# Four edits to a planned two-layer decoder trunk: parameters added later, 32 warm-ups, a cast on VectorE, a lead of 50 for three modulation vectors

## The chip, the cores and the metric

The kernel runs on one core of a Trainium2 chip. The core has five engines with queues of their own: TensorE (PE, matmuls; its weight loads are listed as PEld), VectorE (DVE), ScalarE (ACT), GpSimd (POOL) and SyncE (SP), which here issues nearly all transfers from the main memory. The metric is the device time of one execution in microseconds; the median of three runs is compared.

## The reference, cut to what matters

One sequence of 256 tokens of width 1024 passes through two layers. Each layer is a half-step SwiGLU feed-forward (width 2816), a mixer, and a second half-step feed-forward. Every sublayer is normalised and modulated by vectors that come from the conditioning vector c; a last norm follows.

```
for l in range(2):
    mod = (silu(c) @ w_mod[l] + b_mod[l]).reshape(9, 1024)         # nine modulation vectors
    h = rmsnorm(x, g[l, 0]) * (1 + mod[1]) + mod[0]
    x = x + 0.5 * mod[2] * swiglu(h, w_ffn1_gu[l], w_ffn1_down[l])
    h = rmsnorm(x, g[l, 1]) * (1 + mod[4]) + mod[3]
    x = x + mod[5] * hybrid_mixer(h, w_in[l], w_out[l], ...)
    h = rmsnorm(x, g[l, 2]) * (1 + mod[7]) + mod[6]
    x = x + 0.5 * mod[8] * swiglu(h, w_ffn2_gu[l], w_ffn2_down[l])
return rmsnorm(x, g_final)
```

The mixer projects h once and feeds three parts: windowed attention (8 query heads, 2 key/value heads, window 128), a gated linear recurrence behind a convolution of 4, and a gated convolution of 3, sb * conv3(sc * sx). Their outputs are concatenated and projected back. All data are float32.

## The kernel before

x is kept transposed, as `xT`, 8 tiles of 128 channels by 256 tokens. Every weight tile is loaded as float32 into a buffer `raw` (three of them) and split in two by `unit` (line 323): ACT casts it to the high half `wH` (line 336), DVE subtracts to get the remainder `wL` (line 341). Eight such pairs can be held (`"w": 8`). The activations are split the same way into `zH`, `zL`, so one product takes three matmuls (`mm3`, lines 348 to 350), or two where both halves of the activation are streamed at once (`mm2`, lines 355 and 356). The weights of a feed-forward come in 11 chunks of 256 columns for gate and up; the first three chunks of the first feed-forward are taken row by row together with the first two modulation vectors, by `first`. `evac` (line 473) and the lines 505 to 518 turn a result into the SwiGLU product; `x_add` (line 491) adds a sublayer's output to x; `make_z` (413, 416) makes the next input. At the end of each sublayer but the last, `stats` (line 445) puts four small matmuls on PE that sum the squares.

A modulation vector is made by `mod_vector`: eight transfers of 512 KB into `mraw` (three buffers), a DVE step for each (lines 373 and 375) into the one buffer `macc`, a reduction (line 379), four small matmuls (line 384) and a last addition (line 387). Vectors 0 and 1 of layer 0 are made by `first` instead; the other 16 are made by this function, in the order of their numbers, since `macc` is one buffer. Of layer l vector 5 gates the mixer's output, 6 and 7 are the shift and scale behind the mixer.

The mixer's convolution part ends in the tile `sp`; its product with sb (line 731) is split into `yo`: a cast on ACT (line 834) and a subtraction on DVE (line 835). These are the last halves that the output projection takes.

`consts` loads the mixers' parameters: seven small transfers (sinks, convolution weights, biases, lambda; `ssum_t` and `sinkb`, line 884) and eight for the block-diagonal gate matrices (`gatew`, line 1048), with a clearing of the gate matrices (line 1040), copies of the position bias on ACT (1052) and some 30 tiny DVE operations for a softplus.

Before the data arrive, `N_WARM` matmuls of a tile of ones run on PE (line 924); each shows as two instructions.

The order of the work on each engine is not written by hand. Every operation is added to a planner with its engine, an estimated duration, what it reads and writes, and for PE the sum of the matmul time added before it (`base`). `due` walks back from the end and gives each operation the latest start `lst` at which nothing behind it is late; `lead` is taken off it. `emit` then simulates the engines: of all operations that are ready and have a buffer it takes the engine that can start first, and on it, of those that start within 0.06 us of the earliest, the one with the smallest `lst`:

```
soon = [c for c in cand if c[0] <= t0 + EAGER]
t1, o = min(soon, key=lambda c: (c[1].lst + 2.0 * (c[0] - t0), c[1].idx))
```

A transfer of over 300 KB is a candidate only once the modelled wire is at most `BACKLOG` = 4 us behind. The order so found is the program order of each engine; on the chip an engine works through it in that order.

Of the kernel before, what the change touches and what calls it, by code (L numbers as in the profile page):

```python
# [8 lines left out]
F32 = mybir.dt.float32  # L9
F32R = mybir.dt.float32r  # L10
ACTF = mybir.ActivationFunctionType
ALU = mybir.AluOpType
# [13 lines left out]
LAT = {("PE", "PE"): 0.002, ("DVE", "DVE"): 0.128, ("ACT", "ACT"): 0.143, ("POOL", "POOL"): 0.1, ("PE", "DVE"): 0.196,  # L26
       ("PE", "ACT"): 0.197, ("DVE", "PE"): 0.177, ("ACT", "PE"): 0.217, ("DVE", "ACT"): 0.128, ("ACT", "DVE"): 0.131,
       ("DVE", "POOL"): 0.2, ("POOL", "DVE"): 0.06}
MOD_LEAD = 8.0
EAGER = 0.06  # L30
MARGIN = 1.0
HOLD = 40.0
LAGS = (0, 1, 5)
BACKLOG = 4.0
N_WARM = 40


class T:
# [15 lines left out]
class Plan:  # L54
# [6 lines left out]
    def add(self, eng, dur, fn, r=(), w=(), base=None, kb=0, lead=0.0):  # L61
        o = Op()
        o.eng, o.dur, o.fn, o.kb, o.idx, o.lead = eng, dur, fn, kb, len(self.ops), lead
        deps, tiles = set(), []
        for key in list(r) + list(w):
            t = key[0] if isinstance(key, tuple) else key
            if isinstance(t, T) and t not in tiles:
                tiles.append(t)
                if not t.ops and not t.loose:
                    self.order.setdefault(t.tag, []).append(t)  # L70
                t.ops.append(o)
        for key in r:
            assert key in self.lastw or key in ("zsH", "zsL") or key[0] == "zS", key
            if key in self.lastw:
                deps.add(self.lastw[key])
            self.readers.setdefault(key, []).append(o)
        for key in w:
            if key in self.lastw:
                deps.add(self.lastw[key])
            deps.update(self.readers.get(key, ()))  # L80
            self.lastw[key] = o
            self.readers[key] = []
        deps.discard(o)
        o.deps, o.tiles = deps, tiles
        if eng == "PE" and base is None:
            o.base = self.pe
            self.pe += dur
        else:
            o.base = base
        self.ops.append(o)  # L90
        return o
# [107 lines left out]
def cd(n):  # L199
    return 0.068 + n / 960.0  # L200


def ca(n, p=0):
    return 0.093 + n / 1200.0 + 0.093 * p
# [3 lines left out]
def trunk(ctx: ExitStack, tc: tile.TileContext, x, c, w_mod, b_mod, g_norm, w_gu1, w_dn1, w_gu2, w_dn2,  # L208
# [6 lines left out]
    V, A, G, PE = nc.vector, nc.scalar, nc.gpsimd, nc.tensor  # L215
    P = Plan()
    add = P.add
# [28 lines left out]
    bT = const.tile([128, NL, 72], F32, name="bT")  # L246
    cact = const.tile([128, KD], F32, name="cact")
    c32 = const.tile([128, KD, 32], F32, name="c32")
    mod = const.tile([128, NL, 72], F32, name="mod")
# [38 lines left out]
    def l_cols(w, l, col):  # L288
        raw = load([(ALLP, v_kc, w[l, :, col:col + 256].rearrange("(k p) c -> p k c", p=128))])
        return [(raw, lambda r, t=t: v_kc(r)[:, :, t * 128:t * 128 + 128], KD, None) for t in range(2)]  # L290
# [70 lines left out]
    def mcol(l, v):  # L361
        return mod[:, l, v * 8:v * 8 + 8]

    def mod_vector(l, v):
        acc, t32, ps = new("macc"), new("t32"), new("s", loose=True)
        for k in range(KD):
            raw = new("mraw")
            add("SP", 0.06, lambda k=k, raw=raw: nc.sync.dma_start(out=raw(), in_=w_mod[l, k * 128:k * 128 + 128, v * D:v * D + D]),
                w=[raw], kb=524.0)

            def go(k=k, raw=raw):
                if k == 0:
                    V.tensor_scalar(out=acc(), in0=raw(), scalar1=cact[:, k:k + 1], scalar2=None, op0=ALU.mult)
                else:
                    V.scalar_tensor_tensor(out=acc(), in0=raw(), scalar=cact[:, k:k + 1], in1=acc(), op0=ALU.mult, op1=ALU.add)  # L375
            add("DVE", 0.66 if k == 0 else 1.2, go, r=[raw, "c"] + ([acc] if k else []), w=[acc])

        def red():
            V.tensor_reduce(out=t32(), in_=acc().rearrange("p (b c) -> p b c", c=32), axis=AX.X, op=ALU.add, apply_transpose=True)

        def mm():
            tv = t32().rearrange("p (k b) -> p b k", b=4)
            for b in range(4):
                PE.matmul(ps()[32 * b:32 * b + 32, 0:8], lhsT=fold, rhs=tv[:, b, :], start=True, stop=True, skip_group_check=True)

        def fin():
            V.tensor_tensor(out=mcol(l, v), in0=ps()[:, 0:8], in1=bT[:, l, v * 8:v * 8 + 8], op=ALU.add)
        add("DVE", 1.14, red, r=[acc], w=[t32])
        add("PE", 0.1, mm, r=[t32, "fold"], w=[ps], base=1e9)
        add("DVE", 0.08, fin, r=[ps, "bT"], w=[("mod", l, v)], lead=MOD_LEAD)  # L390


    def prep(l, s):
# [101 lines left out]
    def ffn(l, s, wg, wd, getR, nxt, first=False, done=None):  # L495
# [27 lines left out]
        for ch in range(11):  # L523
            if first and ch < 3:
                if ch:
                    continue
                pss, prods = [new("gu") for _ in range(3)], {}
                for k in range(KD):
                    if k % 2 == 0:
                        first(k // 2, prods)  # L530
                        if k == 4:
                            R = getR()
                    ws = [unit(u) for u in l_rows(wg, l, k)]
                    for m in range(6):
                        def go(m=m, k=k, ws=ws, pss=pss):
                            for i in range(2):
                                mm3(pss[m // 2]()[:, m % 2, i * S:i * S + S], ws[i], m, zH[:, k, 0:S], zL[:, k, 0:S],
                                    k == 0 and i == 0, k == KD - 1)
                        prods[k, m] = add("PE", 2 * C3, go, r=[(w, j) for w in ws for j in range(2)] + [("zH", k), ("zL", k)],
                                          w=[(pss[m // 2], m % 2)])  # L540
                consts()
                for m in range(6):
                    put(m, pss[m // 2], R, m % 2)
                continue
            ug, uu = l_cols(wg, l, ch * 256), l_cols(wg, l, FF + ch * 256)
            for t in range(2):
                m = ch * 2 + t
                ps = pair([unit(ug[t]), unit(uu[t])])
                if R is None:
                    R = getR()  # L550
                put(m, ps, R)
# [3 lines left out]
            r=[("mod", l, 3 * s + 2)], w=[gv])  # L555
        a = prep(*nxt) if nxt else None
        ssum = new("ssum")
        for dp in range(4):
            pss = [new("gu"), new("gu")]
            f0 = 0  # L560
            for ci, n in enumerate((8, 8, 6)):
                us = l_down(wd, l, f0, n, dp * 256)
                for t in range(2):
                    w, ps = unit(us[t]), pss[t]
# [22 lines left out]
    def mixer(l, getR, nxt):  # L587
# [13 lines left out]
        ps = P2(l_cols(w_in, l, 512))  # L601
# [148 lines left out]
        for g in range(2):  # L750
            ps = new("s")
# [55 lines left out]
        sp = new("big")  # L807
# [23 lines left out]
        for i in range(2):  # L831
            add("DVE", 0.4, lambda i=i, t=t: stt(sp()[:, 2 + i, :], t()[:, i, 0:S], t()[:, i, 256:257], sp()[:, 2 + i, :], ALU.add, ALU.mult),
                r=[t], w=[(sp, 2 + i)])
        add("ACT", ca(512), lambda: A.copy(yo()[:, 0, 0:2, :], sp()[:, 2:4, :]), r=[(sp, 2), (sp, 3)], w=[(yo, 0, 0)])  # L834
        add("DVE", cd(512), lambda: V.tensor_tensor(out=yo()[:, 1, 0:2, :], in0=sp()[:, 2:4, :], in1=yo().bitcast(F32)[:, 0, 0:2, :],  # L835
                                                    op=ALU.subtract), r=[(sp, 2), (sp, 3), (yo, 0, 0)], w=[(yo, 1, 0)])

        acc = [new("gu"), new("gu")]

# [255 lines left out]
    fin = {}  # L1095
# [27 lines left out]
    add("ACT", ca(256), lambda: A.copy(RM(), psm()[:, 0:256]), r=[psm], w=[RM], base=E0)  # L1123

    for l, v in [(0, v) for v in range(2, 9)] + [(1, v) for v in range(9)]:
        mod_vector(l, v)
    s0 = ffn(0, 0, w_gu1, w_dn1, lambda: spread(r0, True), (0, 1), first=first)
    s1 = mixer(0, lambda: spread(stats(s0)), (0, 2))
    s2 = ffn(0, 2, w_gu2, w_dn2, lambda: spread(stats(s1)), (1, 0))
# [61 lines left out]
```

## Time and profile before

| | |
|---|---|
| median of 3 runs | 976.43 us (974.82 to 977.58) |
| profiled execution | 980.18 us, span 978.4 us |
| PE busy | 959.5 us, 98% of the span |
| PE weight loads busy | 907.1 us, 93% |
| DVE busy | 803.5 us, 82% |
| ACT busy | 501.1 us, 51% |
| moved from main memory | 240.52 MB, 247 GB/s over the span |

Matmuls are pipelined, so a PE that shows as busy may still be waiting a little; the number of matmuls that a stretch starts tells more than its busy time. The times of rows count from the start of the span. In a timeline row the first number is the start, the second the duration, and what stands in brackets is how long the engine had been idle and what ended that. The granted clock of PE stands as a share of full speed.

### The profile page before, as it was taken

The page shows a single profiled execution, that of the slowest core. Times are in us where ns is not written, and L with a number is a line of the kernel's source. Part 1 is how long each engine was busy: PE and PEld are TensorE (multiplying, and loading weights), DVE is VectorE, ACT ScalarE, POOL GpSimd, SP SyncE. Part 2 cuts the span into 40 slices and gives each one's busy share as a digit, 9 for nine tenths or more (in the row PEclk, how much of TensorE's full clock was granted, in tenths as well). Part 3 has the DMA queues.
Part 4 walks back from the last instruction along what each step waited for, and adds up shares of the span by engine and source line. Part 5 has one row for each costly group of instructions (what it writes and reads, how often), then busy time and mean ns, then how long its engine had stood idle before and what let it go on. Part 6 is the DMA issues. An engine that isn't in the chain of part 4 may idle for free.

```text
span 978.4 us, 18188 instructions
## 1 busy us (share of the span) xinstructions
PE 959.5 (98%) x7407; PEld 907.1 (93%) x7407; DVE 803.5 (82%) x1211; ACT 501.1 (51%) x773; POOL 11.4 (1%) x16
## 2 busy tenths in 40 slices
PE   8999999999999999999999999999999999999997
PEld 7889999889888999998899999988998999999886
DVE  5688999999899999989789976677999989666651
ACT  4436554445955554544454554444577555544431
POOL 1000000000000000000000000000000000000000
PEclk9999999999999999999999999999999999999999
DMA  9976789998856889997878965598784777656521
GB/s 329 348 254 225 262 294 328 345 306 307 206 174 236 295 272 325 306 319 252 297 226 295 309 205 182 194 314 252 251 233 172 254 246 247 208 183 192 164 76 44
DMA packets 185783, 242.75 MB, mean 248 GB/s; under 512 B 6504, under 2 KB 164452, under 8 KB 185700
## 3 DMA queue, kind: packets, MB, share of 16 engines
q1 hardware_dynamic: 185160, 240.96, 75.3%
q8 instruction: 58, 0.95, 0.4%
q10 hardware_dynamic: 540, 0.63, 0.2%
q14 instruction: 25, 0.20, 0.1%
HBM read 240.52 MB, written 1.05 MB: 247 GB/s over the span
## 4 chain that ended last, share of the span: by engine, by line
PE 88%; DVE 7%; DMA 3%; issue 1%; ACT 0%; ACTq 0%; DVEq 0%; POOLq 0%
PE gu L348 20%; PE gu L350 20%; PE gu L349 20%; PE gu L356 15%; PE gu L355 8%; DMA mraw_t<-in_w_mod_dram 2%; DVE wL L341 2%; DVE macc_t L375 1%; DVE xT L491 1%; PE s L986 1%; PE gu L924 1%; DMA sq_t<-in_b_mod_dram 1%; DVE hp_t L731 1%; DMA raw_t<-in_w_ffn_gu_dram 1%; DVE big_t L657 0%
## 5 line engine op out<-in xcount | busy, mean ns | idle before, releaser
L348 PE MATMUL gu<-zH,wH 128*128 128x258 f32 (+1 forms) x1664 | 473.4, 284 | 2.7 <-DVE ev_t L473 1.9
L336 ACT CAST wH<-raw_t 128x1024 fp32r<-128x1024 f32 (+1 forms) x324 | 320.3, 1015 | 301.1 <-PE gu L356 114.8
L350 PE MATMUL gu<-zH,wL 128*128 128x258 f32 (+1 forms) x1664 | 471.1, 283 | 1.2 <-DVE wL L341 1.2
L349 PE MATMUL gu<-zL,wH 128*128 128x258 f32 (+1 forms) x1664 | 469.4, 282 | 0.7 <-DVE zL L416 0.3
L341 DVE TENSOR_TENSOR wL<-raw_t,wH 128x1024 fp32r<-128x1024 f32 (+1 forms) x324 | 375.1, 1181 | 56.3 <-ACT wH L336 54.8
L348 PEld LDWEIGHTS gu<-zH,wH 128*128 128x128 f32 x1664 | 315.3, 189 | 6.2 <-issue 2.5
L349 PEld LDWEIGHTS gu<-zL,wH 128*128 128x128 f32 x1664 | 315.6, 190 | 2.0 <-DVE zL L416 1.5
L350 PEld LDWEIGHTS gu<-zH,wL 128*128 128x128 f32 x1664 | 314.5, 189 | 1.6 <-DVE wL L341 1.6
L356 PE MATMUL gu<-hp_t,wH 128*128 128x512 f32 x704 | 248.0, 393 | 0.0
L355 PE MATMUL gu<-hp_t,wL 128*128 128x256 f32 x704 | 200.4, 285 | 1.8 <-DVE xT L491 1.8
L356 PEld LDWEIGHTS gu<-hp_t,wH 128*128 128x128 f32 x704 | 132.2, 188 | 29.7
L375 DVE SCALAR_TENSOR_TENSOR macc_t<-mraw_t,cact,macc_t 128x1024 f32<-128x1024 f32 x112 | 143.3, 1279 | 6.9 <-DMA mraw_t<-in_w_mod_dram 6.6
L355 PEld LDWEIGHTS gu<-hp_t,wL 128*128 128x128 f32 x704 | 132.3, 188 | 2.5 <-PE gu L356 1.2
L473 DVE TENSOR_TENSOR ev_t<-gu,Rb 128x514 f32<-128x514 f32 x98 | 67.6, 690 | 47.9 <-PE gu L350 47.2
L517 ACT CAST hp_t<-h_t 128x256 fp32r<-128x256 f32 x88 | 35.5, 405 | 73.8 <-DVE h_t L515 73.8
L513 ACT ACTIVATE sg_t<-ev_t 128x256 f32<-128x256 f32 x88 | 44.1, 502 | 41.4 <-DVE ev_t L473 33.2
L491 DVE SCALAR_TENSOR_TENSOR xT<-gu,gv_t,xT 128x256 f32<-128x256 f32 x80 | 36.8, 479 | 17.6 <-PE gu L356 16.0
L518 DVE TENSOR_TENSOR hp_t<-h_t,hp_t 128x256 fp32r<-128x256 f32 x88 | 36.9, 420 | 8.9 <-ACT hp_t L517 8.5
L515 DVE SCALAR_TENSOR_TENSOR h_t<-ev_t,sg_t 128x256 f32<-128x256 f32 x88 | 41.7, 475 | 0.8 <-ACT sg_t L513 0.5
L349 PE MATMUL gu<-hp_t,wH 128*128 128x256 f32 x128 | 36.9, 288 | 1.8 <-DVE hp_t L835 1.8
L348 PE MATMUL gu<-hp_t,wH 128*128 128x256 f32 x128 | 37.8, 295 | 0.2 <-ACT hp_t L834 0.2
L350 PE MATMUL gu<-hp_t,wL 128*128 128x256 f32 x128 | 36.7, 286 | 0.0
(168 smaller groups left out, 487.7 us busy)
## 6 DMA issues: line engine op xcount, KB each, us to landing
raw_t<-in_w_ffn_gu_dram SPq DMA_DIRECT2D x82, 1024.0 KB, 7.2
mraw_t<-in_w_mod_dram SPq DMA_DIRECT2D x128, 512.0 KB, 5.6
raw_t<-in_w_ffn_down_dram SPq DMA_DIRECT2D x32, 1024.0 KB, 5.3
raw_t<-in_w_ffn_down_dram SPq DMA_DIRECT2D x16, 768.0 KB, 6.3
raw_t<-in_w_in_dram SPq DMA_DIRECT2D x12, 1024.0 KB, 5.8
hp_t<-in_w_mod_dram SPq DMA_DIRECT2D x8, 1024.0 KB, 10.8
raw_t<-in_w_ffn_gu_dram SPq DMA_DIRECT2D x16, 384.0 KB, 8.9
raw_t<-in_w_in_dram SPq DMA_DIRECT2D x8, 512.0 KB, 7.0
```

The source lines that it names most:

```text
L336: A.copy(dst(0), view(raw()))
L341: V.tensor_tensor(out=dst(1), in0=view(raw()), in1=h, op=ALU.subtract)
L348: PE.matmul(ps, lhsT=wh[:, wi, :], rhs=aH, start=first, stop=False, skip_group_check=True)
L349: PE.matmul(ps, lhsT=wh[:, wi, :], rhs=aL, start=False, stop=False, skip_group_check=True)
L350: PE.matmul(ps, lhsT=wl[:, wi, :], rhs=aH, start=False, stop=last, skip_group_check=True)
L355: PE.matmul(ps[:, 0:S], lhsT=wl[:, wi, :], rhs=a[:, 0, :], start=first, stop=False, skip_group_check=True)
L356: PE.matmul(ps, lhsT=wh[:, wi, :], rhs=a, start=False, stop=last, skip_group_check=True)
L375: V.scalar_tensor_tensor(out=acc(), in0=raw(), scalar=cact[:, k:k + 1], in1=acc(), op0=ALU.mult, op1=ALU.add)
L473: V.tensor_tensor(out=t()[:, :, 0:257], in0=ps()[:, :, 0:257], in1=Rb[:, R, 0:257].unsqueeze(1).to_broadcast([128, 2, 257]), op=ALU.mult)
L491: add("DVE", 0.4, lambda: V.scalar_tensor_tensor(out=xT[:, d, :], in0=src(), scalar=gv()[:, d:d + 1], in1=xT[:, d, :], op0=ALU.mult, op1=A ...
L513: add("ACT", ca(S, 1), lambda: A.activation(out=sg(), in_=t()[:, 0, 0:S], func=ACTF.Silu, bias=bg_()), r=[t], w=[sg])
L515: add("DVE", 0.4, lambda: V.scalar_tensor_tensor(out=h(), in0=t()[:, 1, 0:S], scalar=bu_(), in1=sg(), op0=ALU.add, op1=ALU.mult), r=[t, sg ...
```

## The change

`consts()` is called before chunk 7 of the first feed-forward's gate and up weights, not after the first three chunks, so its operations are added later and its due times are later by the matmul time of the four chunks between. `N_WARM` falls from 40 to 32. In the mixer the cast of the convolution half moves from ACT to DVE, as a copy that is planned together with the subtraction behind it as one operation, `cut`. `mod_vector` gets its lead as an argument: 50 for the vectors 5, 6 and 7 of both layers, 8 as before for the others.

```diff
--- before.py
+++ after.py
@@ -26,13 +26,13 @@
 LAT = {("PE", "PE"): 0.002, ("DVE", "DVE"): 0.128, ("ACT", "ACT"): 0.143, ("POOL", "POOL"): 0.1, ("PE", "DVE"): 0.196,
        ("PE", "ACT"): 0.197, ("DVE", "PE"): 0.177, ("ACT", "PE"): 0.217, ("DVE", "ACT"): 0.128, ("ACT", "DVE"): 0.131,
        ("DVE", "POOL"): 0.2, ("POOL", "DVE"): 0.06}
-MOD_LEAD = 8.0
+MOD_LEAD, AHEAD = 8.0, 50.0
 EAGER = 0.06
 MARGIN = 1.0
 HOLD = 40.0
 LAGS = (0, 1, 5)
 BACKLOG = 4.0
-N_WARM = 40
+N_WARM = 32
 
 
 class T:
@@ -361,7 +361,7 @@
     def mcol(l, v):
         return mod[:, l, v * 8:v * 8 + 8]
 
-    def mod_vector(l, v):
+    def mod_vector(l, v, lead):
         acc, t32, ps = new("macc"), new("t32"), new("s", loose=True)
         for k in range(KD):
             raw = new("mraw")
@@ -387,7 +387,7 @@
             V.tensor_tensor(out=mcol(l, v), in0=ps()[:, 0:8], in1=bT[:, l, v * 8:v * 8 + 8], op=ALU.add)
         add("DVE", 1.14, red, r=[acc], w=[t32])
         add("PE", 0.1, mm, r=[t32, "fold"], w=[ps], base=1e9)
-        add("DVE", 0.08, fin, r=[ps, "bT"], w=[("mod", l, v)], lead=MOD_LEAD)
+        add("DVE", 0.08, fin, r=[ps, "bT"], w=[("mod", l, v)], lead=lead)
 
 
     def prep(l, s):
@@ -538,10 +538,11 @@
                                     k == 0 and i == 0, k == KD - 1)
                         prods[k, m] = add("PE", 2 * C3, go, r=[(w, j) for w in ws for j in range(2)] + [("zH", k), ("zL", k)],
                                           w=[(pss[m // 2], m % 2)])
-                consts()
                 for m in range(6):
                     put(m, pss[m // 2], R, m % 2)
                 continue
+            if first and ch == 7:
+                consts()
             ug, uu = l_cols(wg, l, ch * 256), l_cols(wg, l, FF + ch * 256)
             for t in range(2):
                 m = ch * 2 + t
@@ -831,9 +832,10 @@
         for i in range(2):
             add("DVE", 0.4, lambda i=i, t=t: stt(sp()[:, 2 + i, :], t()[:, i, 0:S], t()[:, i, 256:257], sp()[:, 2 + i, :], ALU.add, ALU.mult),
                 r=[t], w=[(sp, 2 + i)])
-        add("ACT", ca(512), lambda: A.copy(yo()[:, 0, 0:2, :], sp()[:, 2:4, :]), r=[(sp, 2), (sp, 3)], w=[(yo, 0, 0)])
-        add("DVE", cd(512), lambda: V.tensor_tensor(out=yo()[:, 1, 0:2, :], in0=sp()[:, 2:4, :], in1=yo().bitcast(F32)[:, 0, 0:2, :],
-                                                    op=ALU.subtract), r=[(sp, 2), (sp, 3), (yo, 0, 0)], w=[(yo, 1, 0)])
+        def cut():
+            V.tensor_copy(yo()[:, 0, 0:2, :], sp()[:, 2:4, :])
+            V.tensor_tensor(out=yo()[:, 1, 0:2, :], in0=sp()[:, 2:4, :], in1=yo().bitcast(F32)[:, 0, 0:2, :], op=ALU.subtract)
+        add("DVE", 2 * cd(512), cut, r=[(sp, 2), (sp, 3)], w=[(yo, 0, 0), (yo, 1, 0)])
 
         acc = [new("gu"), new("gu")]
 
@@ -1123,7 +1125,7 @@
     add("ACT", ca(256), lambda: A.copy(RM(), psm()[:, 0:256]), r=[psm], w=[RM], base=E0)
 
     for l, v in [(0, v) for v in range(2, 9)] + [(1, v) for v in range(9)]:
-        mod_vector(l, v)
+        mod_vector(l, v, AHEAD if v in (5, 6, 7) else MOD_LEAD)
     s0 = ffn(0, 0, w_gu1, w_dn1, lambda: spread(r0, True), (0, 1), first=first)
     s1 = mixer(0, lambda: spread(stats(s0)), (0, 2))
     s2 = ffn(0, 2, w_gu2, w_dn2, lambda: spread(stats(s1)), (1, 0))
```

## Rows read from the trace of the kernel before

**Rows 1.** Busy time by engine in two stretches; clock, DMA share and GB/s last

```profile
...
100.00:125.00 25.00, 25.00 (x211) 25.00 (x210) 23.46 (x30) 12.95 (x19) 0.00 (x0) 1.00 0.88 291
...
250.00:275.00 25.00, 23.14 (x178) 20.71 (x177) 22.42 (x60) 24.28 (x60) 0.00 (x0) 1.00 0.64 173
```

**Rows 2.** The chain that ended last: the matmuls of `stats`

```profile
...
226.81 0.34 PE s L445 x4
...
317.82 0.34 PE s L445 x4
...
700.13 0.34 PE s L445 x4
...
784.82 0.34 PE s L445 x4
```

**Rows 3.** Timeline of 262 to 266 us

```profile
...
263.67 1.28 DVE L375 SCALAR_TENSOR_TENSOR macc_t<-mraw_t,cact,macc_t 128x1024 f32<-128x1024 f32 x1 [2.58 <-DMA mraw_t<-in_w_mod_dram]
...
265.61 0.39 PE L348 MATMUL gu<-zH,wH 128*128 128x258 f32 x1 [1.86 <-DVE ev_t L473]
```

**Rows 4.** Timeline of 299 to 305 us

```profile
...
301.18 2.35 DVE L341 TENSOR_TENSOR wL<-raw_t,wH 128x1024 fp32r<-128x1024 f32 x2
...
301.29 0.62 ACT L834 CAST hp_t<-big_t 128x512 fp32r<-128x512 f32 x1 [1.33 <-DVE big_t L731]
...
303.45 0.68 DVE L835 TENSOR_TENSOR hp_t<-big_t,hp_t 128x512 fp32r<-128x512 f32 x1
...
304.19 0.39 PE L349 MATMUL gu<-hp_t,wH 128*128 128x256 f32 x1 [1.84 <-DVE hp_t L835]
```

**Rows 5.** PE alone in stretches of 2 us: busy, granted clock, DMA share

```profile
...
8.00:10.00 2.00, 1.00 (x10) 1.00 1.09 335
...
66.00:68.00 2.00, 2.00 (x12) 0.52 1.07 374
...
304.00:306.00 2.00, 1.81 (x11) 0.75 0.62 203
306.00:308.00 2.00, 2.00 (x12) 0.50 1.00 339
```

**Rows 6.** Timeline of PE near 64 us

```profile
...
64.43 0.38 PE L348 MATMUL gu<-zH,wH 128*128 128x258 f32 x1 [0.85 <-ACT wH L336]
...
65.69 0.38 PE L350 MATMUL gu<-zH,wL 128*128 128x258 f32 x1 [0.76 <-DVE wL L341]
```

**Rows 7.** Timeline of SP's queue, 45 to 66 us

```profile
...
47.39 1.44 SPq L884 DMA_DIRECT2D ssum_t<-in_lru_conv_w_dram  x1
...
57.80 0.40 SPq L272 DMA_DIRECT2D raw_t<-in_w_ffn_gu_dram  x1
58.24 1.36 SPq L1048 DMA_DIRECT2D gatew<-in_lru_gate_a_w_dram  x2
```

**Rows 8.** What SP's queue waited for, 45 to 70 us: total, times, longest

```profile
...
SPq L884 <- DMA mraw_t<-in_w_mod_dram: 3.5, 2, 2.5
```

**Rows 9.** Timeline of the first 20 us

```profile
...
1.99 0.91 DVE L1040 MEMSET gatew<- 128x1024 f32 x1 [0.16 <-issue]
...
15.64 3.62 PE L924 MATMUL gu<-ones 128*128 128x128 f32 x30
...
17.83 1.82 DVE L341 TENSOR_TENSOR wL<-raw_t,wH 128x768 fp32r<-128x768 f32 x2
...
19.34 0.47 PE L348 MATMUL gu<-zH,wH 128*128 128x256 f32 x1
```

**Rows 10.** Groups by line and shape: busy and mean ns, idle time before

```profile
...
L336 ACT CAST wH<-raw_t 128x1024 fp32r<-128x1024 f32 x276 | 280.6, 1047 | 231.0 <-PE gu L349 79.5 <-PE gu L356 68.7 <-DMA raw_t<-in_w_ffn_gu_dram 51.9
...
L1017 DVE CAST zH<-h_t 128x256 fp32r<-128x256 f32 x8 | 2.4, 295 | 0.3
```

**Rows 11.** Timeline of DVE: the reductions of layer 0's vectors 5 and 7

```profile
...
234.82 1.24 DVE L379 TRANSPOSE_TENSOR_REDUCE t_t<-macc_t 128x32 f32<-128x1024 f32 x1
...
296.68 1.25 DVE L379 TRANSPOSE_TENSOR_REDUCE t_t<-macc_t 128x32 f32<-128x1024 f32 x1
```

## The prediction

> **What bounds the kernel now.** I first read the table of stretches. From 75 us on, in most stretches, TensorE (PE) starts 211 matmuls in 25 us, one every 0.118 us, and its load column is full [rows 1]: that is its pace, and there the time is PE's own. Only stretches that start fewer such matmuls for no reason of their own can be shortened. VectorE (DVE) is close behind: 23.46 us of 25 in the same stretch. So DVE work that is moved has to find room; it is never free before the end of the first mixer.
>
> The chain that ended last gives marks at the end of each sublayer, the matmuls of `stats` [rows 2]. The first mixer lies between 226.81 and 317.82 us, 91.0 us; the second between 700.13 and 784.82, 84.7 us. The work is the same, so the first mixer loses 6.3 us more. The timelines say where. At 263.67 a step of a modulation vector stands at the head of DVE's queue and waits 2.58 us for its piece of `w_mod`; the evacuation behind it is late, and PE stands 1.86 us at 265.61 [rows 3]. At 301.29 ScalarE (ACT) casts the convolution half; DVE, which could not yet subtract, has taken two weight remainders (2.35 us), the subtraction comes at 303.45, and PE stands 1.84 us at 304.19 [rows 4]. After that the granted clock is 0.75 and then 0.50 for two microseconds each [rows 5], the lower of its two levels (1.2 GHz instead of 2.4) for part of the first stretch and all of the second: 0.5 + 1.0 = 1.5 us of matmul time lost. These three make 5.2 of the 6.3 us.
>
> The other loss is near 64 us. PE stands at 64.4 and again 0.76 us at 65.69 [rows 6], about 1.6 us together, and then runs at 0.52 from 66 to 68 [rows 5], 0.96 us more: some 2.6 us at least. The weights it waits for were issued at 57.80, behind the mixers' parameters that begin at 47.39 [rows 7]. In those small transfers SP's queue stood 3.5 us for earlier `w_mod` pieces to land [rows 8].
>
> **The change, part by part.** *Parameters later.* `consts()` moves behind four chunks of the feed-forward, and the planner's due times for it move with it. By its words SP's 64 us stall should go. I don't think it does. A due time only ranks operations that can start at the same moment; an engine with nothing else ready takes what is there. The trace shows this habit: DVE clears the gate matrices at 1.99 us [rows 9], though the mixer needs them after 226. The small transfers still depend only on the last piece of z (`zL`,7), and when that is planned SP's only other candidates are big loads without a free buffer. So I expect the seven small transfers and the eight of the gates where they are, and take 0. If they do move, the gain is the 2.6 us above and what of the low clock lies behind 68, say 3.3. At the other end, the eight gate issues (1.36 us for two [rows 7], 5.5 for all) would stand ahead of weights in the middle of the feed-forward, where up to eight prepared weight tiles cover them (the store of `w` tiles in the planner's table; two remainders take 2.35 us [rows 4], so eight are 9.4 us of DVE's work ahead). That bound is +1 us. The some 30 tiny DVE operations and the two table loads of the softplus only change place; PE doesn't stand between 75 and 250 us, so 0.
>
> *Fewer warm-ups.* A warm-up is two instructions; the last block of 30 runs 15.64 to 19.26 [rows 9], 0.12 us each. Sixteen fewer end it 1.9 us sooner, near 17.4. But the first product also needs the weight remainder, and DVE delivers two of these between 17.83 and 19.65 [rows 9], the first at about 18.74. The first real matmul, now at 19.34, can come some 0.6 us sooner, and the sixth, which needs the second remainder, about 0.3. I take -0.3; the later pieces of that stage come from DMA, so it may also be 0. The gap that opens is about 1.3 us. From 8 to 10 us PE was busy 1.00 of 2.00 us and the clock stayed at 1.00 [rows 5], so I add nothing for the clock. Here the Trainium skill speaks against the edit ("TensorE: Matmul & The Clock Gate", Part 1): its rule is that the low clock is the default state and activity releases it, so filler matmuls taken away can be paid for with slow real ones. By that rule the sum would be about 1.5 us worse, as after 304 us; by the row at 8 to 10 it isn't.
>
> *Convolution halves on DVE.* In each mixer the ACT cast (0.62 us [rows 4]) goes and a DVE copy of 128x512 comes. DVE's cast of 128x256 takes 0.295 us [rows 10], so the copy takes between 0.30 and 0.59; I take 0.45. Copy and subtraction are now one planned unit, so nothing slips between them: 301.26 + 0.45 + 0.68 is about 302.3 instead of 304.13, 1.8 us sooner. With that gap mostly gone the clock should not fall: 1.5 more. The two remainders come 1.1 us later, ahead of weights that PE takes only some microseconds on; with z's chain on DVE right behind I give 0.5 back. Net -2.8 in the first mixer, and 0 in the second, where PE did not wait for the subtraction. Bounds: -3.3, and +0.9 (two copies as pure addition).
>
> *Long lead for vectors 5 to 7.* Nothing is removed: a vector stays eight steps of up to 1.28 us [rows 3] and a reduction of 1.24 [rows 11], some 11 us on DVE, and eight transfers. Today vector 5's reduction is at 234.82 and vector 7's at 296.68 [rows 11], inside the mixer. A lead of 50 instead of 8 puts vector 7's due time near 258, vector 6's near 247, vector 5's near 236. Vector 5 is there already. Vectors 6 and 7 now rank ahead of the mixer's softmax and convolution and of weights that aren't needed at once. Gain: no vector with a near due time in the last 40 us of the mixer and no step with a late transfer in front of an evacuation; the 1.86 us at 265.61 and up to 1.0 of the unexplained rest, -2.9. Cost: today six of vector 6's eight steps are done by 261 (the step at 263.67 is its seventh). If vectors 6 and 7 were done by then, ten steps and two reductions, 12.8 + 2.5 = 15.3 us, would come forward. The weight tiles prepared ahead (ACT waits for PE to free them for most of its idle time [rows 10], so the store is full) cover 9.4 us. The rest, 5.9 us, would fall on the mixer's own chain, and PE would stand. The transfers hold it down: there are three buffers for the pieces, and a step already waits 2.58 us for one today [rows 3]. While a step's piece is missing the planner gives DVE to the chain. So I expect a third of it, +2.0. Net -0.9, between -2.9 and +5.9. In the second mixer vectors 6 and 7 start well before the mixer, so there is room: -0.3.
>
> **Sum.** 0 - 0.3 - 2.8 - 0.9 - 0.3 = -4.3 us. The profiled execution took 980.18 us (span 978.4 and 1.8 around it), so it would take 975.9. It lay 3.75 us above the median of the runs, 976.43; the prediction is made for the median: 972.1.
>
> **Rivals.**
> 1. *Vectors in front of the mixer's chain (slower).* Place: DVE between 235 and 262 us. If all 15.3 us come forward, PE stands 5.9 us at the first transpose of the probabilities, and the clock falls once more (1.5). The later gaps (5.2) then partly vanish, but the planner has fewer tiles ready too; I credit 3. With -0.6 from the warm-ups and the second mixer: 976.4 + 7.4 - 3 - 0.6 = 980.2. It decides from the point where the vectors take over 9.4 us of DVE more than today before 262 us. For it: strict ranking by due time, and DVE at 22.42 of 25 us there [rows 1]. Against: transfers feed the steps too slowly.
> 2. *The parameters really move.* The 3.3 us at 64 us are saved as well: 972.1 - 3.3 = 968.8. For it: any shift of the plan that frees a weight buffer at that moment lets a big load, now due earlier, go first. Against: the ranking as told above.
> 3. *DVE is the bound, and gaps only wander.* Every gain in the first mixer is taken back by DVE at its end: about 976.
> 4. *The clock at the start.* The gap before 19 us lets the clock fall: 972.1 + 0.3 + 1.5 = 973.9. The row at 8 to 10 us speaks against it. The Trainium skill's rule cited above ("TensorE: Matmul & The Clock Gate", Part 1) speaks for it.
>
> **Chances.** The forecast 0.44 (its own range 968 to 976), the slower rival 0.21, parameters moved 0.18, gaps wander 0.09, cold start 0.08. About 0.3% (2.9 us) is what a measurement of this kernel can tell from no change, so faster means below 973.5 and slower above 979.3. Faster: 0.33 from the forecast, 0.17 from rival 2, 0.02 from rival 4, together 0.52. Slower: 0.15 from rival 1, 0.03 from the forecast's upper tail and 0.02 from rival 3. The same: the remaining 0.28. The range must reach both rivals and their bounds: 963 to 982.
>
> **What would show each step.** Parameters: SP's issues of `conv_w` and of the gates still between 47 and 64 us, and the gap near 64. Warm-ups: 64 instead of 80 instructions, first real matmul before 19.1, clock 1.00 up to 60. Convolution: DVE copy and subtraction adjacent, no PE gap of over 0.6 us at that point, no 0.50 clock behind it. Lead: the reductions of vectors 6 and 7 of the first layer before 270 us, and the first mixer shorter than 88 us between its marks. The prediction is wrong if that mixer stays near 91 us or grows, with PE waiting in front of the probabilities' transposes, or if the gap near 64 us is gone.

## The result, and the profile after

The changed kernel takes 986.12 us (median; 984.89 to 986.33) beside 977.0 for the kernel before (four runs; the 976.43 further up is of the first three): ratio 1.0094, interval 1.0081 to 1.0107, some 9 us slower. The forecast was 972.1, range 963 to 982.

First the stretches of [rows 1]. The feed-forward runs as before, 212 matmuls in 25 us. The first mixer's middle starts 129 instead of 178, and part of it has a lower clock.

```profile
100.00:125.00 25.00, 25.00 (x212) 25.00 (x211) 23.53 (x38) 14.14 (x21) 0.00 (x0) 1.00 0.94 307
250.00:275.00 25.00, 17.33 (x129) 15.55 (x128) 22.89 (x60) 18.54 (x51) 0.00 (x0) 0.86 0.71 229
```

The marks of [rows 2], here from the timeline, which reads each 0.16 us earlier than the chain does:

```profile
224.36 0.50 PE L445 MATMUL s<-cmean,ssum_t 128*128 128x1 f32 x4
...
321.09 0.50 PE L445 MATMUL s<-cmean,ssum_t 128*128 128x1 f32 x4
...
698.37 0.50 PE L445 MATMUL s<-cmean,ssum_t 128*128 128x1 f32 x4
...
791.11 0.50 PE L445 MATMUL s<-cmean,ssum_t 128*128 128x1 f32 x4
```

The first mixer takes 96.7 us instead of 91.0, the second 92.7 instead of 84.7. Not all of that is loss, since the planner puts some matmuls of the next feed-forward ahead of the mark: between the two marks of the first mixer the trace holds 594 weight products now and 576 before, of the second 600 and 588 (one of 512 columns counted as two). At 0.118 us [rows 1] that is 2.1 and 1.4 us, so the mixers lose 3.6 and 6.6 us. The head is no shorter than in kernels without the lead: its first mark, 224.36, lies among theirs (223.60 to 224.77), while the profiled execution of before had a head some 2 us longer (226.65). A profile shows one execution, and that one took 980.18 us: near 64 us its PE stood twice and its clock fell [rows 5, 6], where each of the 13 other profiles of this case has one stand of 0.86 or 0.87 us and a clock of 1.00.

The place of the first loss, on PE:

```profile
251.54 1.13 PE L636 MATMUL gu<-hp_t 64*128 64x256 f32 x8
253.37 1.97 PE L756 MATMUL s<-hp_t,gatew 128*128 128x256 f32 x8 [0.69 <-issue]
261.23 0.29 PE L384 MATMUL s<-t_t,fold 128*32 128x8 f32 x8 [5.89 <-ACT big_t L663]
262.61 0.58 PE L348 MATMUL gu<-zH,wH 128*128 128x258 f32 x1 [1.09 <-DVE sm_t L658]
```

And on DVE, the same stretch:

```profile
255.44 1.28 DVE L375 SCALAR_TENSOR_TENSOR macc_t<-mraw_t,cact,macc_t 128x1024 f32<-128x1024 f32 x1 [0.65 <-DMA mraw_t<-in_w_mod_dram]
256.64 0.35 DVE L658 CUSTOM_DVE_ANT_0 big_t<-gu,abias,nsink 128x128 f32<-128x128 f32 x1
...
256.91 1.28 DVE L375 SCALAR_TENSOR_TENSOR macc_t<-mraw_t,cact,macc_t 128x1024 f32<-128x1024 f32 x1
...
258.38 1.28 DVE L375 SCALAR_TENSOR_TENSOR macc_t<-mraw_t,cact,macc_t 128x1024 f32<-128x1024 f32 x1
...
259.84 1.24 DVE L379 TRANSPOSE_TENSOR_REDUCE t_t<-macc_t 128x32 f32<-128x1024 f32 x1
...
262.20 0.35 DVE L658 CUSTOM_DVE_ANT_0 big_t<-gu,abias,nsink 128x128 f32<-128x128 f32 x1
```

L658 (L657 before) is the first step of the softmax. It takes a head's scores out of the PSUM tile `gu` that L636 (L635) wrote, and there are three such tiles. DVE alternates: a step of vector 7, one head, a step, a head. Until the eighth head is read the tile isn't free, and the next projection (L348 at 262.61) needs it. PE has put scores and gate products behind it by 255.34 and stands for 7 us. In the kernel before, the eighth head on DVE, then the gate products and the next projection on PE:

```profile
252.22 0.35 DVE L657 CUSTOM_DVE_ANT_0 big_t<-gu,abias,nsink 128x128 f32<-128x128 f32 x1
```

```profile
253.93 1.99 PE L755 MATMUL s<-hp_t,gatew 128*128 128x256 f32 x8
255.57 0.47 PE L348 MATMUL gu<-zH,wH 128*128 128x258 f32 x1
```

There the tile was free at 252.57, and the projection began at 255.57 without a wait. By these rows the eighth head could have come some 3.0 us later at no cost.

The fold of vector 7 (L384) stands in PE's queue ahead of that projection and waits for the reduction at 259.84; the profile names an ACT operation there, but the fold starts 0.15 us after the reduction's end, 261.08 (0.14 and 0.15 us after it in the kernels with the lead alone and with layer 0's lead alone). (By the Trainium skill, "TensorE: Matmul & The Clock Gate", Step-by-step: what each phase is for, matmuls keep program order; no row here speaks against it: the projection starts behind the fold.) PE's clock, by stretches of 2 us:

```profile
256.00:258.00 2.00, 0.00 (x0) 1.00 0.70 252
258.00:260.00 2.00, 0.00 (x0) 0.67 0.98 320
260.00:262.00 2.00, 0.29 (x8) 0.50 0.89 346
...
264.00:266.00 2.00, 2.00 (x13) 0.62 0.09 33
266.00:268.00 2.00, 2.00 (x19) 1.00 0.00 0
```

The second mixer repeats it. PE stands at the fold and at the projection; the clock is 0.78 from 732 to 734 us and 0.50 from 734 to 736. PE first, then DVE:

```profile
726.33 1.97 PE L756 MATMUL s<-hp_t,gatew 128*128 128x256 f32 x8
731.45 0.25 PE L384 MATMUL s<-t_t,fold 128*32 128x8 f32 x8 [3.15 <-DVE t_t L379]
733.59 0.58 PE L348 MATMUL gu<-zH,wH 128*128 128x258 f32 x1 [1.90 <-DVE sm_t L658]
```

```profile
727.73 1.28 DVE L375 SCALAR_TENSOR_TENSOR macc_t<-mraw_t,cact,macc_t 128x1024 f32<-128x1024 f32 x1 [1.21 <-DMA mraw_t<-in_w_mod_dram]
...
730.06 1.24 DVE L379 TRANSPOSE_TENSOR_REDUCE t_t<-macc_t 128x32 f32<-128x1024 f32 x1
731.23 0.31 DVE L658 CUSTOM_DVE_ANT_0 big_t<-gu,abias,nsink 128x128 f32<-128x128 f32 x1
...
733.19 0.34 DVE L658 CUSTOM_DVE_ANT_0 big_t<-gu,abias,nsink 128x128 f32<-128x128 f32 x1
```

Here all of vector 7 stands ahead of the first head, and DVE itself waits 1.21 us for its last piece.

The rows that answer to [rows 6, 7, 9] are nearly the old ones. The parameters are issued where they were, the gap near 64 us is one of 0.87 us by its row, and the first real matmul comes at 17.59:

```profile
46.83 0.50 SPq L886 DMA_DIRECT2D ssum_t<-in_lru_conv_w_dram  x1
...
54.78 1.36 SPq L1050 DMA_DIRECT2D gatew<-in_lru_gate_a_w_dram  x2
```

```profile
15.62 1.83 PE L926 MATMUL gu<-ones 128*128 128x128 f32 x14
...
17.59 0.41 PE L348 MATMUL gu<-zH,wH 128*128 128x256 f32 x1
...
18.82 0.39 PE L350 MATMUL gu<-zH,wL 128*128 128x256 f32 x1 [0.48 <-DVE wL L341]
...
64.36 0.39 PE L350 MATMUL gu<-zH,wL 128*128 128x258 f32 x1 [0.87 <-DVE wL L341]
```

### The profile page after: what moved, and what is told of

It is laid out like the page before. It is cut to its first block, busy times and chain, and to the rows that moved or that the text cites. A ratio compares the mean times of both kernels' runs of the same rounds, so it can differ in the third digit from the quotient of the medians.

```text
span 984.1 us, 18156 instructions
## 1 busy us (share of the span) xinstructions
PE 957.6 (97%) x7391; PEld 905.2 (92%) x7391; DVE 804.0 (82%) x1213; ACT 500.7 (51%) x771; POOL 10.4 (1%) x16
## 3 DMA queue, kind: packets, MB, share of 16 engines
q1 hardware_dynamic: 185160, 240.96, 74.8%
## 4 chain that ended last, share of the span: by engine, by line
PE 84%; DVE 6%; DMA 5%; ACT 3%; issue 1%; ACTq 0%; POOL 0%; SPq 0%; DVEq 0%; POOLq 0%
PE gu L348 19%; PE gu L350 19%; PE gu L349 19%; PE gu L356 17%; PE gu L355 9%; DMA mraw_t<-in_w_mod_dram 2%; DMA raw_t<-in_w_out_dram 2%; DVE wL L341 1%; DVE macc_t L375 1%; DMA raw_t<-in_w_in_dram 1%; PE s L988 1%; ACT wH L336 1%; ACT big_t L663 1%; DVE hp_t L732 0%; DVE big_t L658 0%
## 5 line engine op out<-in xcount | busy, mean ns | idle before, releaser
L348 PE MATMUL gu<-zH,wH 128*128 128x258 f32 (+1 forms) x1664 | 473.9, 285 | 3.0 <-DVE sm_t L658 3.0
L348 PEld LDWEIGHTS gu<-zH,wH 128*128 128x128 f32 x1664 | 315.9, 190 | 6.1 <-DVE sm_t L658 3.2
L348 PE MATMUL gu<-hp_t,wH 128*128 128x256 f32 x128 | 36.4, 284 | 0.3 <-ACT hp_t L822 0.3
```

The source lines that it names most:

```text
L348: PE.matmul(ps, lhsT=wh[:, wi, :], rhs=aH, start=first, stop=False, skip_group_check=True)
```

## The experiments

Ratios are to the kernel before on the same chip. "Steps" are vector steps plus reductions on DVE between the first mark of a mixer and its eighth softmax instruction, counted in the trace; "eighth" is how long after the mark that instruction starts. The median and the ratio are of all runs; what stands to the right of them is of the one profiled execution. The three kernels with layer 0's lead of 50 have first mixers of 94.9, 96.7 and 97.9 us, so a difference of a microsecond or two between two such figures shows nothing.

| kernel | median us | ratio (interval) | mixers, us | steps, first mixer | eighth | steps, second | eighth |
|---|---|---|---|---|---|---|---|
| before | 976.0 to 977.0 | 1 | 91.0, 84.7 | 5+1 | 25.6 | 5+1 | 25.0 |
| changed | 986.12 | 1.0094 (1.0081, 1.0107) | 96.7, 92.7 | 14+2 | 37.8 | 10+2 | 34.8 |
| lead alone | 986.98 | 1.0103 (1.0087, 1.0119) | 94.9, 92.4 | 14+2 | 36.9 | 10+2 | 33.6 |
| all but the lead | 975.18 | 0.9984 (0.9975, 0.9993) | 89.9, 84.8 | 5+1 | 25.6 | 5+1 | 25.0 |
| cut alone | 975.93 | 0.9990 (0.9981, 0.9998) | 91.1, 84.8 | 5+1 | 25.6 | 5+1 | 25.0 |
| parameters alone | 976.79 | 1.0004 (0.9995, 1.0013) | 90.8, 84.7 | 5+1 | 25.6 | 5+1 | 25.0 |
| lead, layer 0 | 979.86 | 1.0040 (1.0025, 1.0056) | 97.9, 84.7 | 14+2 | 39.2 | 5+1 | 25.0 |
| lead, layer 1 | 983.42 | 1.0069 (1.0054, 1.0085) | 91.5, 91.5 | 5+1 | 25.6 | 10+2 | 33.4 |
| lead 25 alone | 981.66 | 1.0042 (1.0026, 1.0057) | 100.4, 85.7 | 7+1 | 25.8 | 6+1 | 24.6 |
| all, lead 100 | 989.78 | 1.0143 (1.0122, 1.0163) | 86.8, 86.7 | 4+0 | 27.6 | 4+0 | 27.5 |
| lead on reductions | 980.00 | 1.0038 (1.0026, 1.0050) | 84.6, 83.9 | 5+1 | 26.4 | 0+1 | 25.7 |
| same, vector 7 | 1002.9 | 1.0265 (1.0248, 1.0283) | 112.6, 92.3 | 14+2 | 39.2 | 10+2 | 32.6 |

**The lead, and everything else.** The diff of the first holds only `AHEAD` and the argument of `mod_vector`; the second is the changed kernel with these lines back.

```diff
-        mod_vector(l, v)
+        mod_vector(l, v, AHEAD if v in (5, 6, 7) else MOD_LEAD)
```

> The kernel before with one edit: lead 50 for vectors 5 to 7. The step of the prediction that gave this edit -0.9 and -0.3 us would have 976 us. If the vectors' DVE steps rank ahead of the mixer's own chain and PE stands for it in both mixers, as the changed kernel's trace suggests (mixers of 96.7 and 92.7 us), both mixers grow by 5 to 9 us each and the run takes 986 to 992 us.

> The changed kernel with the lead back at 8 for all vectors; the other three edits stay. By the prediction's other terms (0 - 0.3 - 2.8) 974 us, by the view that the changed kernel's loss is the lead's alone also some 2 to 4 us faster than before. If one of the other edits costs, slower than before.

Measured 986.98 and 975.18. The lead costs 1.03% and the other three edits bring 0.16% together; their sum, +8.5 us, is the change's 9 within the intervals.

**The lead by layers.** The condition gets `l == 0 and`, or `l == 1 and`, in front.

> The kernel before with the lead of 50 for vectors 5 to 7 of layer 0 alone. Theory (each layer's lead makes its own mixer longer, by vector steps in front of that mixer's softmax): first mixer 94 to 96 us, second 84 to 85.5, and since the feed-forward behind the first mixer gives 2 to 3 us back, a ratio of 1.001 to 1.004. Rival (one layer's lead upsets the plan of all that follows): second mixer over 88 us too.

> The kernel before with the lead of 50 for vectors 5 to 7 of layer 1 alone. Theory: first mixer 90 to 92 us as before, second 91 to 93, ratio 1.006 to 1.009. Rival (the second mixer's loss in the changed kernel comes from what the first layer's lead moved): second mixer within 1 us of 84.7 and a ratio of 1.000.

Measured +0.40% and +0.69%: 3.9 and 6.7 us, together 1.09% beside 1.03% for both at once. Each layer's lead makes its own mixer longer and leaves the other as it was: with layer 0's the first takes 97.9 us and the second 84.7, with layer 1's 91.5 and 91.5 (91.0 and 84.7 before). Of the 3.2 us that the stretch between the next two marks gives back, 2.8 are 24 products that were already done ahead of the mixer's last mark: they were never lost.

**Which wait: the softmax or the fold.** Vector 7's reduction alone gets a lead, of 42, its last addition keeps 8; so its fold goes elsewhere in PE's queue.

```diff
-        add("DVE", 1.14, red, r=[acc], w=[t32])
+        add("DVE", 1.14, red, r=[acc], w=[t32], lead=lead - MOD_LEAD)
...
-        mod_vector(l, v)
+        mod_vector(l, v, AHEAD if v == 7 else MOD_LEAD)
```

> The kernel before with 42 us of lead on the reduction of vector 7 alone; the single buffer macc pulls vectors 5 and 6 along on DVE, while the folds on PE and the last additions keep 8. DVE's order in the mixers is that of the long lead but for the tiny additions; the fold of vector 7 no longer stands on PE between the gate products and the next projection. Theory A (DVE's steps in front of the scores' softmax, whose PSUM tile the next projection needs): PE still stands 5 us and more in each mixer at that projection, released by DVE's softmax, and the time is 983 to 988 us. Theory B (PE waits for the fold): gaps under 2 us, 975 to 979 us.

The timeline of this kernel's PE:

```profile
254.76 0.25 PE L384 MATMUL s<-t_t,fold 128*32 128x8 f32 x8
...
264.59 0.58 PE L348 MATMUL gu<-zH,wH 128*128 128x258 f32 x1 [9.58 <-DVE sm_t L657]
```

No waiting fold stands ahead of the projection here (the one at 254.76 is vector 6's, reduced at 240.58), and PE stands 9.58 us all the same, until DVE has read the eighth head. So the order on DVE sets this wait in the first mixer; the fold only stood in front of it. In the second mixer PE stands 1.95 us at the projection and 1.46 us ahead of the gate products (744.76), not the 5 that theory A asked for; the eighth head comes 32.6 us after the mark and the mixer is as long as with the lead alone (92.3 us), but which wait costs how much there isn't shown. The total, 1002.9, lies outside both ranges and isn't a measure of either theory: further gaps follow at 288.72, 293.98 and 302.34 us, as vector 5's last addition, due late, holds one of the two PSUM tiles `s` (PE waits for that addition at 288.72; the rest is read from the order and was not tried).

The same lead on the reductions of all three vectors was meant to leave the fold alone in the same way:

> The kernel before with the long lead put on the vectors' reduction on DVE, while the fold matmuls on PE and the last addition keep a lead of 8. Theory A, DVE's order (the vector's steps stand in front of the scores' softmax, whose PSUM tile the next projection needs): as slow as with the lead alone, 986 to 992 us, PE gaps of 5 us and more in both mixers. Theory B, PE's order (the fold matmul is planned early and PE waits in its queue for the reduction): the gaps go and the time is 974 to 979 us.

It was no clean test. Leads on reductions add up along the one buffer `macc` (42 on vector 7's is passed on to 6's, and so on), so the vectors ran far earlier: vector 5's reduction at 171.19 us instead of 234.82, and the debt fell into the feed-forward ahead of the mark, which came at 237.07. The two mixers were then the shortest of all, 84.6 and 83.9 us.

**How much lead.** First 25 in the place of 50, with no other edit, then 100 in the changed kernel.

```diff
-MOD_LEAD, AHEAD = 8.0, 50.0
+MOD_LEAD, AHEAD = 8.0, 25.0
```

> The kernel before with a lead of 25 for vectors 5 to 7. Due times then lie some 25 us later than with 50, behind the first scores' softmax. Theory A: most of the loss is gone, 976 to 981 us, vector 7's reduction some 10 to 20 us later than with 50. If any lead above 8 costs in proportion, some 981 us.

> All four edits, but with a lead of 100 in the place of 50. By its program order DVE has 52 vector steps behind it at the first softmax and none between the first softmax and the twelfth; in the changed kernel it is 44 and two more between, in the kernel before 33 and one. Theory A (a softmax instruction is late because vector steps are taken in front of it within the mixer): the steps now lie in the feed-forward before, the first mixer comes out below 93 us, without a gap of over 4 us at the projection behind the softmax, and any cost lies ahead of the mark at 224 us. Rival (each vector step taken before the mixer's softmax, wherever, costs the mixer its prepared tiles): the first mixer is longer than the 96.7 us of the changed kernel.

The counts in the expectation for lead 100 took merged rows as one; by the trace DVE has 52 steps behind it at the first softmax, in the changed kernel 46 and two more between, before 35 and one. With 25, ten steps and a reduction fall between the eighth and the last softmax instruction of the first mixer (four steps before), and PE stands at the transposes of the probabilities (L696) and again at 289.75 and 293.32:

```profile
266.04 1.94 PE L696 MATMUL gu<-ident,big_t 128*128 128x128 f32 x8 [4.02 <-DVE sm_t L657]
```

```profile
289.75 1.98 PE L715 MATMUL s<-big_t,hp_t 128*64 128x256 f32 x8 [3.33 <-ACT big_t L701]
...
293.32 0.58 PE L348 MATMUL gu<-hp_t,wH 128*128 128x256 f32 x1 [1.60 <-ACT hp_t L821]
```

The run with 25 takes 981.66 us, what "in proportion" expected and just above theory A's range: the second mixer's loss is nearly gone (85.7 us), the first's isn't. The 100.4 us overstate the first mixer, since the profiled execution took 985.46 us, the longest of its four, and PE's clock was 0.50 from 290 to 298.

With 100 the steps lie ahead of the mark, and both mixers take under 87 us with no stand behind the softmax, though 606 products lie between the marks of each. The mark itself comes at 240.02 instead of 224.36: DVE owes weight remainders in the feed-forward now. Three of PE's waits, and two stretches of that kernel (in them the kernel before starts 175 and 145 matmuls at a clock of 1.00):

```profile
172.49 0.38 PE L355 MATMUL gu<-hp_t,wL 128*128 128x256 f32 x1 [3.62 <-DVE wL L341]
...
178.06 0.58 PE L355 MATMUL gu<-hp_t,wL 128*128 128x256 f32 x1 [1.78 <-DVE wL L341]
...
187.84 0.39 PE L355 MATMUL gu<-hp_t,wL 128*128 128x256 f32 x1 [1.73 <-DVE wL L341]
```

```profile
150.00:175.00 25.00, 20.35 (x134) 17.80 (x132) 22.73 (x30) 11.12 (x17) 0.00 (x0) 0.97 0.95 328
175.00:200.00 25.00, 21.32 (x102) 17.72 (x102) 23.53 (x27) 5.98 (x7) 0.00 (x0) 0.83 0.94 323
```

**The cut alone.** The kernel before with `cut` in the place of the two operations.

```diff
-        add("ACT", ca(512), lambda: A.copy(yo()[:, 0, 0:2, :], sp()[:, 2:4, :]), r=[(sp, 2), (sp, 3)], w=[(yo, 0, 0)])
...
+        add("DVE", 2 * cd(512), cut, r=[(sp, 2), (sp, 3)], w=[(yo, 0, 0), (yo, 1, 0)])
```

> The kernel before with one edit: the convolution half's cast on DVE. By the prediction -2.8 us, 974 us, with PE's 1.84 us gap at the subtraction in the first mixer and the low clock behind it gone. If DVE is the bound there, no change (within 1 us).

DVE in this kernel, then PE, in the stretch of [rows 4]:

```profile
298.60 0.88 DVE L731 SCALAR_TENSOR_TENSOR big_t<-ev_t,big_t 128x256 f32<-128x256 f32 x2
299.39 1.22 DVE L341 TENSOR_TENSOR wL<-raw_t,wH 128x1024 fp32r<-128x1024 f32 x1
300.52 0.42 DVE L835 CAST hp_t<-big_t 128x512 fp32r<-128x512 f32 x1
300.98 0.69 DVE L836 TENSOR_TENSOR hp_t<-big_t,hp_t 128x512 fp32r<-128x512 f32 x1
```

```profile
301.09 0.35 PE L348 MATMUL gu<-hp_t,wH 128*128 128x256 f32 x1 [1.10 <-DVE hp_t L835]
301.73 0.38 PE L349 MATMUL gu<-hp_t,wH 128*128 128x256 f32 x1 [0.28 <-DVE hp_t L836]
```

The copy takes 0.42 and the subtraction of the same shape 0.69 us. (The Trainium skill, "VectorE: DVE Perf Modes", The perf-mode tier table, lets a float32 copy run in a mode of twice the pace, and an operation on two tensors not; these rows agree, with a fixed part on top: from 256 to 512 columns the copy grows from 0.295 [rows 10] to 0.42, the operation on two tensors from 0.42, line 518's mean, to 0.69.) One remainder (1.22 us) still slips in between product and copy, PE stands 1.1 + 0.28 instead of 1.84 us, and the clock is 1.00 from 300 to 306 us. Yet the mixer is 91.1 us long, as before. Counted by weight products since the mark, this execution comes to the cut 0.8 us behind the kernel before, wins 1.9 us over the next 48 products, and loses 1.2 over the 24 behind these, where PE waits for DVE's `zL`. The first 0.8 are not the cut's: the stand of [rows 3] is 2.15 us here and the clock falls behind it, as it didn't in the profile of before, and a stand of 1.02 us at a fold is missing. PE and its clock in this kernel:

```profile
263.33 0.39 PE L348 MATMUL gu<-zH,wH 128*128 128x258 f32 x1 [2.15 <-DVE ev_t L473]
...
310.39 0.39 PE L349 MATMUL gu<-zL,wH 128*128 128x258 f32 x1 [0.55 <-DVE zL L416]
```

```profile
264.00:266.00 2.00, 2.00 (x13) 0.58 0.60 225
266.00:268.00 2.00, 2.00 (x12) 0.57 0.00 0
```

The 0.1% that the run shows is at the edge of its interval.

**The parameters alone.** The call of `consts()` is moved, nothing else.

> The kernel before with the parameters' loading moved alone. The prediction put this at 0: SP's order keeps conv_w and the gates between 47 and 64 us. Expected: ratio between 0.9985 and 1.0010, conv_w issued at 47 to 48 us. The rival (the parameters really move out of the feed-forward's start) expects 2.6 to 3.3 us less, a ratio of 0.9966 to 0.9973, and conv_w after 64 us. The first mixer should stay within 1 us of the 91.0 us of before; if it comes out at 89 to 90 us, the move of the due times, not the cut, is what shortened it in the kernel with all edits but the lead.

Measured 1.0004: no effect. `conv_w` is issued at 47.76 us, and the first mixer keeps its 91 us, so the rival (conv_w after 64 us, 2.6 to 3.3 us less) falls.

**Towards a better version.** Without the lead there remain stands in the first mixer. Two trials on the kernel with all but the lead: a third buffer for the reductions' results, and the lead on the reductions of layer 1 only.

```diff
-        "macc": 1, "t16": 4, "t32": 2, "r": 4, "a": 4, "gv": 2, "sm": 3}
+        "macc": 1, "t16": 4, "t32": 3, "r": 4, "a": 4, "gv": 2, "sm": 3}
```

> The changed kernel without the long lead and with three t32 buffers instead of two, so that layer 1's vector 4 can be reduced before vector 2's fold at 634 us and vector 5's steps can use DVE's idle time between 560 and 635 us. If the vectors crowd layer 1 because of that buffer, the second feed-forward pair and the second mixer lose 2 to 4 us: 971 to 973.5 us against 975.2 without. If DVE is no bound in layer 1, no change, 975.

```diff
-        add("DVE", 1.14, red, r=[acc], w=[t32])
+        add("DVE", 1.14, red, r=[acc], w=[t32], lead=lead - MOD_LEAD)
...
-        mod_vector(l, v)
+        mod_vector(l, v, AHEAD if l == 1 and v in (5, 6, 7) else MOD_LEAD)
```

> The changed kernel with the long lead on the reductions of vectors 5 to 7 of layer 1 alone (the leads add up along the chain of vectors, so they fall far ahead of the mixer) and 8 elsewhere. In the run with that lead in both layers, layer 1 took 462.7 us between its marks against 467.0 before. So 972 us against 975.2 if that holds by itself; 975 or more if it was the first layer's debt that made it.

Measured 974.37 (0.9975; 0.9965 to 0.9985) and 974.77 (0.9981; 0.9972 to 0.9989). Both are quicker than either kernel of this case, and neither can be told from all but the lead (0.9984; 0.9975 to 0.9993): what these two edits add isn't shown.

## Why the prediction was wrong

**The lead in the first mixer** was put at -0.9 us and is +3.9. The step that failed is "a third of it": the prediction worked out that 15.3 us of vector work could come forward and that 9.4 of them would be covered, and then let the transfers hold two thirds of the rest back. They held back little. In the changed kernel nine more steps and one more reduction stand ahead of the eighth softmax (14+2 against 5+1), 9 x 1.28 + 1.24 = 12.8 us, and that instruction comes 12.3 us later after the mark. DVE waited for a piece twice on the way, 0.62 us at 240.96 and 0.65 at 255.44. The planner did not leave DVE to the mixer's chain between two pieces: it took one head each time and went back to the vector. The cover was wrong too. Prepared weights don't help a PE that waits for a PSUM tile; what covered the delay was the 3.0 us between the eighth head and the next projection, and PE's own coming there 1.7 us later after the mark. The stands of [rows 3] and [rows 4] and the low clock behind them did go, 5.2 us, and so did two that the prediction had not found, 1.02 us at a fold and 0.19 at 301.97:

```profile
289.58 0.25 PE L384 MATMUL s<-t_t,fold 128*32 128x8 f32 x8 [1.02 <-DVE hp_t L727]
```

In their place are 7.7 us of stand at 253 to 262 (0.69, and 255.34 to 262.61 without the fold's 0.29), 1.3 of low clock up to 266 (13 matmuls instead of 19 in the last 2 us, half pace in the 1.4 before), 1.4 in the waits at 287.74 and 289.22, 0.32 and 1.09, and 0.5 at 232.78. That makes +4.5, where the marks give 3.6 and the layer-0 run 3.9; the rest was not followed. The 6.3 us that the first mixer was said to lose were a little more: by the counts of products above, the second holds 12 more between its marks, 1.4 us.

**The lead in the second mixer** was put at -0.3 ("there is room") and is +6.7. This is the largest error, outside every bound that was written down. The step that failed is the reading "vectors 6 and 7 start well before the mixer". Vector 6 does start ahead of that mixer, in both kernels, but vector 7 in neither: its first step is at 731.14 us before, behind the softmax's eighth instruction (724.94), and at 707.72 now, ahead of the first (731.23). Five steps and a reduction more, 7.6 us, and the eighth softmax instruction 9.8 us later, with 1.21 us of it DVE's own wait for a piece. The second mixer had next to no stands to win back (0.31 us), so what is lost counts in full: 3.15 and 1.90 us of stand and some 1.5 of low clock make 6.5 of the 6.6 that the marks give.

**Rival 1** was right in mechanism and sign, and its condition held (over 9.4 us more of vector work on DVE by 262 us: 12.8). Its 980.2 is too low by the second mixer, which it had at -0.3: with +6.7 there it would be 987.2. Its place was nearly right. It named the transposes of the probabilities; with a lead of 25 the stand is there (4.02 us), with 50 it is one step earlier, at the projection that needs the scores' PSUM tile. DVE's order is the cause in both.

**The cut** was put at -2.8 and measures -1.0 (interval -1.9 to -0.2). Copy and subtraction take 0.42 + 0.69 us as foreseen, and the clock stays up behind them; that nothing slips in holds only between those two, not between product and copy. And of the 1.9 us won there 1.2 were gone 24 products later, at DVE's `zL`, which is rival 3's mechanism. In the changed kernel itself PE doesn't wait at this place at all.

**The parameters** at 0 were right: conv_w at 46.83, the gates from 54.78, the gap near 64 still there, and 1.0004 alone. The 2.6 us that the prediction saw lost near 64 us were in good part that one execution's: its second stand (0.76 us) and its low clock are in no other profile. **The warm-ups** at -0.3 fit what is left of all but the lead (0.9984) beside the cut (0.9990) and the parameters (1.0004), -1.0 us with about as much uncertainty; alone they weren't run. The traces show the size: the stand near 64 us ends at 64.31 to 64.39 in the five kernels with 32 warm-ups and at 64.63 to 64.82 in the eight others with 40 that have one such stand, the parameters alone being the latest. There are 64 instructions, the first real matmul is at 17.59 (under 19.1), and the clock is 1.00 from 8 to 60 us, so rival 4 falls. The first product did not need the remainder, as the prediction had it; the third did, at 18.82. By the Trainium skill ("TensorE: Matmul & The Clock Gate", Part 1) filler taken away could have been paid for in slow matmuls; here the trace does not show that.

## What to carry to other kernels

A lead in a planner's due times is not slack: everything due early is put ahead of everything due on time, so work that is needed only later is done in front of the chain that somebody waits for. Before moving such work, count what stands on the same engine between the start of a stage and the first instruction that frees a buffer for the bounding engine; here 12.8 and 7.6 us moved into that stretch made that instruction 12.3 and 9.8 us later. What of it reaches the end depends on how long the bounding engine can do without the buffer and on what stands it had there before. Where two stages look alike, work out the second as well; here the one that "had room" lost most.

## What the runs showed of the hardware that wasn't expected

PE's granted clock fell while it stood in the first mixer: 1.00 from 256 to 258 us, 0.67 in the next two and 0.50 after that, and it was back at 1.00 from 266, with PE at work since 262.61. Behind much shorter stands it went either way: near 64 us it fell to 0.52 in the kernel before [rows 5] (0.85 and 0.76 us), but in the changed kernel it stayed at 1.00 from 64 to 68 (0.87 us). In the first mixer it fell behind 2.15 us at 263.33 with the cut alone, and not behind 2.35 us at the same place, 263.49, with layer 1's lead. So one profile of one execution doesn't tell what a stand costs in clock. At the very start PE was slow in both kernels: the first twelve warm-ups took 2.93 us, the twelve from 8.78 us (9.15 before) 1.55. DVE's cast of 128x512 took 0.42 us where ACT's took 0.62 [rows 4].
